# Which queue carries the loads: SyncE and ACT swap roles in a 180-degree image rotation

## The chip, the cores and the metric

The kernel runs on one core of a Trainium2 chip. DMA transfers are issued from SyncE and from ACT (ScalarE), each through a queue of its own: on the profile's page q1 is SyncE's queue and q10 is ACT's (50.07 and 0.26 MB in the kernel before). VectorE does the copies. The metric is device time in microseconds (us); the profiled span is about 1.8 us shorter. The kernel before takes 122.06 us (median of 3 runs, 121.93 to 122.1).

## The reference

```python
def setup_inputs():
    batch, c, h, w = 32, 3, 256, 256
    return {"x": np.random.randn(batch, c, h, w).astype(np.float32)}

def reference(x):
    return np.rot90(x, k=2, axes=(-2, -1)).astype(np.float32)
```

A rotation by 180 degrees reverses each of the 96 planes of 65,536 floats from end to end: 25.17 MB in, 25.17 MB out, no arithmetic.

## The kernel before

The planes are taken in three groups of 32, A, B and C. Each plane is cut into four strips of 64 KB, so a group fills 128 partitions with 64 KB each. VectorE reverses each strip in place, through a scratch tile, in 12 copies, and the store writes the four strips of a plane in reverse order.

```python
    def load(t, g, lo, hi, queue=nc.sync):
        return queue.dma_start(out=t[:, lo:hi], in_=x4[g][:, lo:hi])
    def store(t, g, lo, hi):
        return nc.sync.dma_start(out=o4[g][:, ::-1, lo:hi], in_=t[:, lo:hi])
    # ... inside(t): the 12 copies ...
    TAIL = 1536
    HEAD = 512
    load(A, 0, 0, HEAD, nc.scalar)          # head: 2 KB a row, on ACT's queue
    load(A, 0, HEAD, E)                     # bulk of A: 62 KB a row
    load(Bt, 1, 0, E)
    body = load(Ct, 2, 0, E - TAIL)
    load(Ct, 2, E - TAIL, E)                # tail: 6 KB a row
    inside(A)
    LEAD = 128
    store(A, 0, 0, LEAD)                    # lead: 512 B a row
    first = store(A, 0, LEAD, E)            # held until body has landed
    # ... the manual dependency of first on body ...
    for g, t in ((1, Bt), (2, Ct)):
        inside(t)
        store(t, g, 0, E)
```

The large store of A waits by hand for the body of C (32.5 us in the profile), so that it doesn't compete with the loads. The small lead and the tail of C bridge the time in which that store is being issued: it is issued at 59.63 us and its first packet starts at 60.84, and the lead's packets start between 60.48 and 61.22.

Of the kernel before, what the change touches and what calls it, by code (L numbers as in the profile page):

```python
# [2 lines left out]

os.environ.setdefault("NEURON_RT_ULTRASERVER_MODE", "4")

# [4 lines left out]


@with_exitstack
def kernel(
    ctx: ExitStack,
    tc: tile.TileContext,
    x: bass.AP,
    out: bass.AP,
):








    nc = tc.nc
    P = 128

    B, C, H, W = x.shape
    L = H * W
    G = 32
    E = L // 4
    J = E // 8

    x4 = x.rearrange("b c h w -> (b c) (h w)").rearrange(
        "(g n) (s e) -> g (n s) e", n=G, s=4)
    o4 = out.rearrange("b c h w -> (b c) (h w)").rearrange(
        "(g n) (s e) -> g n s e", n=G, s=4)  # L40

    pool = ctx.enter_context(tc.tile_pool(name="slots", bufs=1))
    A = pool.tile([P, E], x.dtype, tag="A")
    Bt = pool.tile([P, E], x.dtype, tag="B")
    Ct = pool.tile([P, E], x.dtype, tag="C")
    T = pool.tile([P, J], x.dtype, tag="T")

    def back(t, lo, hi):
        return t[:, hi - 1:(lo - 1 if lo else None):-1]

    def copy(dst, src):
        tc.keep_in_program_order(nc.vector.tensor_copy(out=dst, in_=src))  # L52

    def load(t, g, lo, hi, queue=nc.sync):
        return queue.dma_start(out=t[:, lo:hi], in_=x4[g][:, lo:hi])  # L55

    def store(t, g, lo, hi):
        return nc.sync.dma_start(
            out=o4[g][:, ::-1, lo:hi], in_=t[:, lo:hi])

    def inside(t):
        for lo in range(0, E // 2, J):
            hi = E - lo - J
            copy(T[:, :], back(t, hi, hi + J))
            copy(t[:, hi:hi + J], back(t, lo, lo + J))
            copy(t[:, lo:lo + J], T[:, :])

    TAIL = 1536
    HEAD = 512
    load(A, 0, 0, HEAD, nc.scalar)  # L70
    load(A, 0, HEAD, E)
    load(Bt, 1, 0, E)
    body = load(Ct, 2, 0, E - TAIL)
    load(Ct, 2, E - TAIL, E)
    inside(A)
    LEAD = 128
    store(A, 0, 0, LEAD)
    first = store(A, 0, LEAD, E)
    tc.add_manual_dep(
        first.ins, body.ins.name,  # L80
        mybir.DependencyInfo(mybir.DependencyClass.Sync, mybir.DependencyReason.DATA),
        reason="the first store is queued while the last strip is on its way")
# [5 lines that stand above are left out]
# [1 line left out]
_INS = ['x']  # L89
_OUTS = [((32, 3, 256, 256), 'float32')]  # L90


# [23 lines left out]
```

## Time and profile before

| | before |
|---|---|
| device time | 122.06 us |
| profiled span | 120.2 us |
| VectorE busy | 44.2 us (37%) |
| data moved | 50.33 MB, 419 GB/s over the span |
| share of queue q1 (SyncE) / q10 (ACT) | 97.0% / 0.6% |

A DMA "packet" in what follows is one row's contiguous piece: the page's 1296 packets are 128 for each of the nine DMAs and 144 under 512 bytes. 128 rows over 16 DMA engines make 8 packets per engine on average for each DMA.

### The profile page before, as it was taken

What the parts mean: (1) busy time and instruction counts of PE and PEld (TensorE: products, weight loads), DVE (VectorE), ACT (ScalarE), POOL (GpSimd) and SP (SyncE); (2) the same over time, 40 slices, a digit from 0 to 9 for tenths busy, and PEclk for the clock granted to TensorE, in tenths of its full rate; (3) what the DMA queues carried; (4) which work ended last, traced back from release to release, by engine and by line L of the source; (5) the groups of instructions that cost most, each with busy time, mean ns of one, the idle gap of its engine ahead of it and who ended that gap; (6) DMA issues with size and microseconds to landing.
All of it is one profiled execution on the core that took longest, in us unless ns stands there. A gap on an engine that the chain in (4) does not pass through costs nothing.

```text
span 120.2 us, 97 instructions
## 1 busy us (share of the span) xinstructions
DVE 44.2 (37%) x36; POOL 0.2 (0%) x4
## 2 busy tenths in 40 slices
DVE  0000000499995099999059999500000000000000
POOL 0000000000000000000000000000000000000000
DMA  9888988899889879979499777988898889888990
GB/s 338 349 349 349 698 349 349 360 654 393 349 349 633 382 316 553 395 316 633 178 452 693 346 346 346 693 349 349 349 698 349 349 349 698 349 349 349 654 393 0
DMA packets 1296, 50.33 MB, mean 419 GB/s; under 512 B 144, under 2 KB 272, under 8 KB 528
## 3 DMA queue, kind: packets, MB, share of 16 engines
q1 hardware_dynamic: 1152, 50.07, 97.0%
q10 hardware_dynamic: 144, 0.26, 0.6%
HBM read 25.17 MB, written 25.17 MB: 419 GB/s over the span
## 4 chain that ended last, share of the span: by engine, by line
DMA 34%; DVE 25%; another core or an unknown queue 4%; issue 1%; SPq 0%; DVEq 0%
DMA Bt<-in_x_dram 34%; DVE T L52 8%; DVE Bt L52 8%; DVE Ct L52 8%; SPq L55 0%; DVEq L52 0%
## 5 line engine op out<-in xcount | busy, mean ns | idle before, releaser
L52 DVE COPY T<-A 128x2048 f32<-128x2048 f32 x4 | 4.9, 1226 | 22.7 <-DMA A<-in_x_dram 22.6
L52 DVE COPY T<-Ct 128x2048 f32<-128x2048 f32 x4 | 4.9, 1227 | 4.5 <-DMA Ct<-in_x_dram 4.4
L52 DVE COPY T<-Bt 128x2048 f32<-128x2048 f32 x4 | 4.9, 1226 | 4.4 <-DMA Bt<-in_x_dram 4.3
L52 DVE COPY Bt<-Bt 128x2048 f32<-128x2048 f32 x4 | 4.9, 1227 | 0.1
L52 DVE COPY A<-A 128x2048 f32<-128x2048 f32 x4 | 4.9, 1227 | 0.1
L52 DVE COPY A<-T 128x2048 f32<-128x2048 f32 x4 | 4.9, 1227 | 0.1
L52 DVE COPY Bt<-T 128x2048 f32<-128x2048 f32 x4 | 4.9, 1227 | 0.1
L52 DVE COPY Ct<-T 128x2048 f32<-128x2048 f32 x4 | 4.9, 1227 | 0.1
L52 DVE COPY Ct<-Ct 128x2048 f32<-128x2048 f32 x4 | 4.9, 1227 | 0.1
L100 POOL MEMSET const-bfloat16-1.0<- 128x1 bf16 x1 | 0.1, 101 | 0.0
L100 POOL MEMSET const-uint8-127<- 128x1 uint8 x1 | 0.1, 101 | 0.0
L100 POOL MEMSET const-float32-0.0<- 128x1 f32 x1 | 0.1, 98 | 0.2 <-issue 0.2
L100 POOL MEMSET const-float32-1.0<- 128x1 f32 x1 | 0.1, 98 | 0.0
## 6 DMA issues: line engine op xcount, KB each, us to landing
out_dram<-A SPq DMA_DIRECT2D x1, 8128.0 KB, 21.1
A<-in_x_dram SPq DMA_DIRECT2D x1, 7936.0 KB, 21.9
Ct<-in_x_dram SPq DMA_DIRECT2D x1, 7424.0 KB, 57.9
Ct<-in_x_dram SPq DMA_DIRECT2D x1, 768.0 KB, 59.3
A<-in_x_dram ACTq DMA_DIRECT2D x1, 256.0 KB, 22.0
out_dram<-A SPq DMA_DIRECT2D x1, 64.0 KB, 35.2
Bt<-in_x_dram SPq DMA_DIRECT2D x1, 40.8
out_dram<-Bt SPq DMA_DIRECT2D x1, 39.8
```

Of the source, the lines that this page charges most:

```text
L52: tc.keep_in_program_order(nc.vector.tensor_copy(out=dst, in_=src))
L100: nc = _bacc.Bacc("TRN2", target_bir_lowering=False, num_devices=1)
```

## The change

The intent is to give loads and stores a queue each, so that no store stands behind a load, as the lead store did for 35.2 us in the kernel before. ACT carries the bulk of the loads, SyncE the head of A and all stores. The calls are pinned in program order, which does not alter the order of the stores.

```diff
-    def load(t, g, lo, hi, queue=nc.sync):
-        return queue.dma_start(out=t[:, lo:hi], in_=x4[g][:, lo:hi])
+    def load(t, g, lo, hi, queue=nc.scalar):
+        return tc.keep_in_program_order(
+            queue.dma_start(out=t[:, lo:hi], in_=x4[g][:, lo:hi]))
 
     def store(t, g, lo, hi):
-        return nc.sync.dma_start(
-            out=o4[g][:, ::-1, lo:hi], in_=t[:, lo:hi])
+        return tc.keep_in_program_order(nc.sync.dma_start(
+            out=o4[g][:, ::-1, lo:hi], in_=t[:, lo:hi]))
...
-    load(A, 0, 0, HEAD, nc.scalar)
+    load(A, 0, 0, HEAD, nc.sync)
```

## The prediction

> **What bounds the kernel now.** I read the page's slices first. VectorE is busy in 44.2 of 120.2 us, only between the first landing and the middle of the run. The DMA engines are busy from end to end:
>
> ```profile
> DVE  0000000499995099999059999500000000000000
> ...
> DMA  9888988899889879979499777988898889888990
> ...
> DMA packets 1296, 50.33 MB, mean 419 GB/s; under 512 B 144, under 2 KB 272, under 8 KB 528
> q1 hardware_dynamic: 1152, 50.07, 97.0%
> q10 hardware_dynamic: 144, 0.26, 0.6%
> ```
>
> q1 is SyncE's queue and carries all but 256 KB; q10 is ACT's and carries only the head (2 KB of each row of group A). A packet's bytes are booked where it starts, which is why slices swing between 178 and 698 GB/s while the digits hardly fall. Is there a hole anywhere? I take the issue starts from the timeline and add the landing times of the page's sixth part:
>
> ```profile
> out_dram<-A SPq DMA_DIRECT2D x1, 8128.0 KB, 21.1
> A<-in_x_dram SPq DMA_DIRECT2D x1, 7936.0 KB, 21.9
> ...
> A<-in_x_dram ACTq DMA_DIRECT2D x1, 256.0 KB, 22.0
> out_dram<-A SPq DMA_DIRECT2D x1, 64.0 KB, 35.2
> Bt<-in_x_dram SPq DMA_DIRECT2D x1, 40.8
> ```
>
> Landings: A 0.73 + 21.9 = 22.6, B 1.18 + 40.8 = 42.0, C's tail 2.1 + 59.3 = 61.4; stores A 59.6 + 21.1 = 80.7, B 60.3 + 39.8 = 100.1, C 76.7 + 42.7 = 119.4. The steps are 19.4, 19.4, 19.3, 19.4 and 19.3 us for 8.39 MB each: 433 GB/s, for loads, for stores, and across the turn from one to the other. So the run is 22.6 (start-up plus the first group) + 5 x 19.36 + 0.8 after the last landing = 120.2. There is no idle stretch to win back except the start-up, 22.6 - 19.4 = 3.2 us. The chain that ended last stops at VectorE's last copy at 76.7; that store then waits behind two others, so the copies are not the limit: C's store is issued at 76.7 and its turn comes at 100.
>
> The waits of SyncE show the timing of the turn:
>
> ```profile
> SPq L58 <- DMA Ct<-in_x_dram: 33.1, 2, 32.5
> ...
> SPq L58 <- DVE A L52: 3.6, 1, 3.6
> ```
>
> The large store of A is held 32.5 us for the body of C, issued at 59.63, and its packets start 1.2 us later. Windows around that point (start:end, length, VectorE, POOL, clock, DMA share, GB/s):
>
> ```profile
> 60.00:60.45 0.45, 0.00 (x0) 0.00 (x0) 1.00 0.98 410
> 60.45:60.84 0.39, 0.00 (x0) 0.00 (x0) 1.00 0.82 313
> 60.84:61.06 0.22, 0.00 (x0) 0.00 (x0) 1.00 7.42 3105
> 61.06:61.26 0.20, 0.00 (x0) 0.00 (x0) 1.00 4.67 1997
> ```
>
> The jump at 60.84 is the first 65,024-byte store packets. Before it the share falls only to 0.82: a few early engines ran dry, for 0.18 x 0.39 = 0.07 us on average. The late engines reached the store only after 61.06, with it already waiting. The late ones set the end.
>
> [...]
>
> ```profile
> DMA packets 16, 1.02 MB, mean 317 GB/s; under 512 B 0, under 2 KB 0, under 8 KB 0
> ...
> q1 hardware_dynamic: 16, 1.02, 94.9%
> ```
>
> That is 1.5 to 4.7 us: one 63,488-byte packet on each of 16 engines and none of the head. From 4.7 to 5.2 us:
>
> ```profile
> q1 hardware_dynamic: 13, 0.83, 380.6%
> q10 hardware_dynamic: 15, 0.03, 15.8%
> ```
>
> Now one head packet per engine goes between two large ones. A head has 8 packets per engine (128 rows over 16), so it needs 8 turns and lands after 22.0 us, with the whole of A (21.9), though 256 KB alone would need 0.6 us at 433 GB/s.
>
> **The change, part by part.** Nothing is removed or added in work. The instruction order shows the same 36 copies on VectorE with the same kinds of wait, and the same nine DMAs of the same sizes: SyncE now has the head and four stores, ACT four loads. The order on SyncE is as before: lead (first 512 B of each row of A), rest of A, B, C. So 50.33 MB at 433 GB/s stay.
>
> (1) *Start.* Both sequencers begin at 0.73 us, ACT's issue takes 0.38 us and SyncE's 0.39, so ACT issues its four loads at the pace at which SyncE did. Each engine still has 8 large and 8 head packets before group B. If SyncE's head wins the first turn, the order in each pair is swapped and the head meets the start-up latency instead of the large packet: 2,048 bytes took 0.08 us in the packet records, so the effect is within +-0.1 us. If ACT's descriptors should come later than SyncE's, the engines pass the time with head packets, 8 x 0.08 = 0.67 us of useful work. Cost 0, at most 0.3.
>
> (2) *The lead store.* Before, it is issued at 26.4 and waits behind B and C in the same queue, until 61.6 (35.2 us). Now its queue is empty, so it takes a turn at once: 8 packets, one for each large load packet (65,536 bytes, 2.42 us), so about 8 x 2.42 = 19.4 us, up to 2.4 more for the first turn. It lands some 20 us after its issue. Its packets are 0.0235 us apart in the packet records, so 8 are 0.19 us per engine: spent in the load phase instead of at the turn. C's body lands 0.2 us later, the turn is 0.2 us shorter: sum 0.
>
> (3) *The turn.* The lead no longer stands between C's tail and the large store. The store is issued at about 59.8 and starts at about 61.0. The tails end, shifted by 0.19, between 60.67 (from 60.48) and 61.24 (from 61.05). The earliest engine now idles some 0.36 us, where before it idled 0.17; the latest has its store waiting, as before. So the end stays, unless the store's arrival slips. On late engines a 6,144-byte tail packet or the tail's completion can be left when the store comes in, and then stands behind one or two packets of 2.4 us. The tail may thus land at 61.6 to 66.5, and VectorE's C copies (15.1 us) end at 77 to 82. C's store has its turn at 100: 18 us of slack. Hidden.
>
> (4) *Stores B and C* queue behind A on SyncE, as now.
>
> Sum: 0 from the data, 0 to +0.3 at the start, 0 to +0.2 at the turn.
>
> **The rivals.** *Turns cost something.* If the switch between two queues cost a gap, or made loads and stores mix badly, the lead's 8 turns would pay it. Against: the head already makes 128 such turns and A's group costs 22.6 us, of which start-up explains the 3.2. At 0.1 us a turn it would be 0.8 us: 122.9. *A bubble at the turn.* If the store's packets came 1 us later through the changed queue, all engines would idle: 123. Against: the same sequencer, the same wait on C's body. *A starved tail.* With the tail's 8 small packets all alternating with 2.4 us stores it would take some 20 us, C would be ready at about 97, still just before 100; only with this and a delay would the end move, by 1 to 3 us. Against: the body's completion and the 1.2 us to the first packet leave at most one tail packet. *A gain.* Earlier stores can't help, because the large store is still held for C's body; a head that hides start-up latency could give 0.1 to 0.3 us, 121.8.
>
> **Range and chances.** The runs before spread over 121.93 to 122.1. I take 122.1, with 121.6 to 122.6 for the small terms and the difference from chip to chip. Over 2% is 2.4 us, more than any rival but two at once: faster 0.01, within 2% 0.97, slower 0.02.
>
> **What would show it.** Span 120.0 to 120.6; q10 carries about 24.9 MB and q1 about 25.4; lead store about 20 us to landing; large store of A issued at 59.7 to 59.9 and landing 21 us on; first copy of A at 22.5 to 22.9; first copy of C at 61.6 to 66.5; C's store landing at 119.3 to 119.8. I am wrong if group A comes 1 us or more late (ACT's issue path), if the steps of 19.36 us change (turns cost), or if the DMA digits show a hole at 58 to 63 us.

## The result, and the profile after

The changed kernel takes 122.59 us (median of 6 runs, 122.29 to 122.71); the kernel before took 122.01 (6 runs, 121.93 to 122.1). The ratio is 1.0045, with a 95% interval of 1.0032 to 1.0058. A ratio is the mean time of one kernel's fast runs over the mean of the other's fast runs of the same rounds, so it is not quite the ratio of the medians. The 0.45%, about 0.55 us, is clear of noise.

The page of the kernel after: busy tenths of the DMA engines in 40 slices, and the two queues (packets, MB, share of the 16 engines' span).

```profile
DMA  8988997899889979979599877988898889888990
...
q1 hardware_dynamic: 720, 25.43, 49.3%
q10 hardware_dynamic: 576, 24.90, 47.9%
```

The traffic is divided as expected and there is still no hole. The page's DMA issues (size, us from issue to landing):

```profile
out_dram<-A SPq DMA_DIRECT2D x1, 8128.0 KB, 21.0
A<-in_x_dram ACTq DMA_DIRECT2D x1, 7936.0 KB, 22.4
...
A<-in_x_dram SPq DMA_DIRECT2D x1, 256.0 KB, 20.0
out_dram<-A SPq DMA_DIRECT2D x1, 64.0 KB, 22.3
Bt<-in_x_dram ACTq DMA_DIRECT2D x1, 41.4
```

The lead store lands 22.3 us after its issue instead of 35.2, so it does go early. But the bulk of A took 22.4 us instead of 21.9, B 41.4 instead of 40.8, and the head landed 2 us sooner (20.0 against 22.0). The delay is there before group A has landed and stays to the end. VectorE's first copy starts at 23.12 instead of 22.62, B's at 42.68 instead of 42.05, C's at 62.12 instead of 61.55.

So I look at the first microseconds. Windows (start:end, length, VectorE, POOL, clock, DMA share, GB/s), first before, then after. A packet's bytes and its whole time are booked where it starts, so a share can exceed 1 and is no measure of how busy the engines are within the window:

```profile
1.50:2.10 0.60, 0.00 (x0) 0.00 (x0) 1.00 4.82 1587
2.10:2.85 0.75, 0.00 (x0) 0.00 (x0) 1.00 0.20 85
2.85:4.00 1.15, 0.00 (x0) 0.00 (x0) 1.00 0.00 0
```

```profile
1.50:2.10 0.60, 0.00 (x0) 0.00 (x0) 1.00 1.23 270
2.10:2.85 0.75, 0.00 (x0) 0.00 (x0) 1.00 2.01 625
2.85:4.00 1.15, 0.00 (x0) 0.00 (x0) 1.00 0.92 392
```

Before, 15 of the 16 first large packets start before 2.10 us (1587 GB/s x 0.60 us = 952 KB, 15 packets of 63,488 bytes). After, they trickle in until past 2.85 us. The queue view of the changed kernel from 1.5 to 4.0 us says what went ahead of them:

```profile
q10 hardware_dynamic: 16, 1.02, 102.0%
q1 hardware_dynamic: 32, 0.07, 30.0%
```

There are 32 head packets, two per engine on average (the records don't name the engine), and one large packet each. Before, the large packet was first on every engine (16 packets on q1 and none on q10 from 1.5 to 4.0 us). The packet records show what the head packets cost here: 0.08 to 1.14 us each (mean 0.38), where a head packet later in the stream takes 0.084. The first large packets start between 2.06 and 3.54 us (mean 2.79), before between 1.76 and 2.82 (mean 1.93).

A second thing in the same lines matters for the account below. The 16 large packets took 102.0% of 2.5 us, 2.55 us on average; before, 94.9% of 3.2 us (the line is in the prediction), 3.04 us. The same size takes 2.34 us later in the stream. So the head packets took a part of the start-up time off the large packets behind them, and the average engine lost little: it begins B at 22.20 instead of 21.98. What grew more is the spread over the engines.

The engines are spread more widely when they begin group B. Windows around that moment, before and after:

```profile
21.62:22.25 0.63, 0.00 (x0) 0.00 (x0) 1.00 4.00 1717
22.25:22.85 0.60, 0.23 (x1) 0.00 (x0) 1.00 0.00 0
```

```profile
21.62:22.25 0.63, 0.00 (x0) 0.00 (x0) 1.00 2.41 1040
22.25:22.85 0.60, 0.00 (x0) 0.00 (x0) 1.00 1.52 655
```

Before, all engines have begun B by 22.25; after, six have not (655 x 0.60 = 393 KB, six packets of 64 KB). By the packet records, the latest engine begins B at 22.75 instead of 22.24, which is 0.51 us later. The end of the last store packet is 119.59 instead of 119.06, which is 0.53 us later. In this profiled run the whole loss is there at 22.75.

The turn to the stores moves with it. Windows of the kernel after:

```profile
60.40:60.84 0.44, 0.00 (x0) 0.00 (x0) 1.00 0.93 391
60.84:61.30 0.46, 0.00 (x0) 0.00 (x0) 1.00 0.42 174
61.30:61.72 0.42, 0.00 (x0) 0.00 (x0) 1.00 5.88 2492
```

The jump of the large store's first packets stands after 61.30 (61.42 by the packet records) instead of at 60.84, since the body of C, for which it waits, is complete only when the latest engine has finished. Just before it the earlier engines ran dry: by the packet records' real times the 16 engines were busy for 0.57 of the window 60.84 to 61.30 (before, for all of it), and from 58 to 64 us each engine idled 0.32 us on average. Is this a second loss, or only the first one seen again? That, and whether the queue split costs anything of itself, is for experiments.

### The profile page after: what moved, and what is told of

Read it like the earlier page. It is cut to its first block, busy times and chain, and to the rows that moved or that the text cites. A ratio compares the mean times of both kernels' runs of the same rounds, so it can differ in the third digit from the quotient of the medians.

```text
span 120.7 us, 97 instructions
## 1 busy us (share of the span) xinstructions
DVE 44.2 (37%) x36; POOL 0.2 (0%) x4
## 2 busy tenths in 40 slices
DMA packets 1296, 50.33 MB, mean 417 GB/s; under 512 B 144, under 2 KB 272, under 8 KB 528
## 4 chain that ended last, share of the span: by engine, by line
DMA 34%; DVE 25%; another core or an unknown queue 3%; issue 1%; ACTq 0%; DVEq 0%
DMA Bt<-in_x_dram 34%; DVE T L52 8%; DVE Ct L52 8%; DVE Bt L52 8%; ACTq L56 0%; DVEq L52 0%
## 6 DMA issues: line engine op xcount, KB each, us to landing
A<-in_x_dram ACTq DMA_DIRECT2D x1, 7936.0 KB, 22.4
Ct<-in_x_dram ACTq DMA_DIRECT2D x1, 768.0 KB, 59.9
out_dram<-A SPq DMA_DIRECT2D x1, 64.0 KB, 22.3
Bt<-in_x_dram ACTq DMA_DIRECT2D x1, 41.4
out_dram<-Bt SPq DMA_DIRECT2D x1, 39.8
```

## The experiments

Theory S is that the loss comes from the start: SyncE's small head packets get to the DMA engines ahead of ACT's large ones. Rival Q is that loads and stores taking turns between two queues cost it. Rival A is that ACT's queue is slow to start by itself. Diffs are against the changed kernel unless said otherwise. All outputs were correct. One execution of each kernel was profiled, and it isn't always a typical one; its time stands in the table at the end of this section. Up to four kernels shared runs of the kernel before (medians 122.02, 122.04 and 122.08).

**Swap without split**

```diff
-        return tc.keep_in_program_order(nc.sync.dma_start(     # in store()
+        return tc.keep_in_program_order(nc.scalar.dma_start(
```

> The swap without the split: head on SyncE, all other loads and all stores on ACT in one queue. Theory S (the 0.6 us arises at the start, because SyncE's head packets reach the DMA engines before ACT's bulk packets): 122.5 to 122.7, first copy of A at 23.1, lead store landing 34 to 36 us after issue. Rival Q (the cost is in loads and stores taking turns between two queues: lead in the load phase, and the turn at 60 us): 122.0, first copy of A at 22.6.

Measured: 122.29 (122.13 to 122.51), ratio 1.0025 (1.0012 to 1.0037), some 0.3 us. The profiled run was the slowest of the set, 122.51. Its queue view from 1.5 to 4.0 us:

```profile
q10 hardware_dynamic: 16, 1.02, 99.6%
q1 hardware_dynamic: 48, 0.10, 32.1%
```

Here it is three head packets per engine on average ahead of the large one, and the first copy of A at 23.21. Loads and stores share one queue, the lead lands 35.2 us after issue as before, and still time is lost. S stands in kind; the size is less than it said, and Q, which said 122.0, can't be the cause of this part.

**Split without swap**

```diff
-    def load(t, g, lo, hi, queue=nc.scalar):
+    def load(t, g, lo, hi, queue=nc.sync):
-        return tc.keep_in_program_order(nc.sync.dma_start(     # in store()
+        return tc.keep_in_program_order(nc.scalar.dma_start(
-    load(A, 0, 0, HEAD, nc.sync)
+    load(A, 0, 0, HEAD, nc.scalar)
```

> The split without the swap: head on ACT and all loads on SyncE as before, only the four stores moved to ACT. Theory S: 121.9 to 122.2, first copy of A at 22.6, although the lead store goes early (about 22 us to landing). Rival Q: 122.5 to 122.7 with the first copy of A still at 22.6 and the loss at 59 to 62 us.

Measured: 122.16 (122.1 to 122.29), ratio 1.0014 (1.0000 to 1.0027). First copy of A at 22.61, lead landing 22.3 us after issue. This is within S's range and far below Q's. The ratio means 0.17 us for the split, and by the interval anything from none to 0.33 us.

**Changed kernel without a head**

```diff
-    load(A, 0, 0, HEAD, nc.sync)
-    load(A, 0, HEAD, E)
+    load(A, 0, 0, E)
```

> The changed kernel with A loaded by one DMA on ACT, no head on SyncE. Theory S: 121.9 to 122.2, first packets of ACT's queue at 1.7 to 2.1 us and first copy at 22.6. Rival A (ACT's queue is slow to deliver its first packets, whatever SyncE does): 122.5, first ACT packets later than 2.1 us and spread, first copy at 23.1. Rival Q: 122.5 with the first copy at 22.6.

Measured: 122.04 (122.04 to 122.17), ratio 1.0005 (0.9992 to 1.0017). The queue view from 1.5 to 4.0 us:

```profile
q10 hardware_dynamic: 16, 1.05, 125.4%
```

ACT's 16 large packets start at 1.74 to 2.15 us when nothing is ahead of them, and the first copy comes at 22.58. ACT's queue is not slow, so A falls. The stores are still in their own queue, the lead still goes early (22.2 us to landing), and the loss is gone to within the interval's 0.2 us, so Q falls again as the main cause.

**Head held back**

```diff
+    nc.gpsimd.memset(A[:, 0:HEAD], 0.0)
     load(A, 0, 0, HEAD, nc.sync)
```

> The changed kernel, but SyncE's head is held back by a GpSimd memset of its 2 KB columns, so that ACT's bulk is first on the engines. Theory S: 121.9 to 122.2, the first packets are 63,488 bytes, first copy of A at 22.6 to 22.8. Rival A: 122.5, ACT's first packets late though alone. Rival Q: 122.5.

Measured: 122.14 (122.06 to 122.37), ratio 1.0014 (1.0001 to 1.0026). The profiled run was the fastest of the set, 122.06. SyncE's issue moves from 0.73 to 1.28 us. The first packets are then 63,488 bytes on every engine (1.74 to 2.57 us), the first copy comes at 22.50, and the time is 0.4 us under the changed kernel's. The same DMAs on the same queues, in the other order, are without most of the loss (the intervals of the two ratios don't meet). The order is the cause of most of it.

**Kernel before without its head** (against the kernel before)

```diff
-    load(A, 0, 0, HEAD, nc.scalar)
-    load(A, 0, HEAD, E)
+    load(A, 0, 0, E)
```

> The kernel before without its head on ACT: A is one DMA on SyncE, everything in one queue. Theory S (only heads that come before the bulk cost anything; the head on ACT in the kernel before is harmless and useless): 121.9 to 122.15, first copy of A at 22.5 to 22.6. Rival H (the head on the other queue won the kernel before something at the start): 122.3 or more, first copy at 22.9.

Measured: 122.06 (121.97 to 122.62), ratio 1.0012 (0.9995 to 1.003). Four of the six runs are at 121.97 to 122.08, two at 122.46 and 122.62. By the median the head in the kernel before is neither gain nor loss. The profiled run was the one of 122.62, and in it one engine began B at 22.52, the next at 22.22, with no small packet at the start; one first packet took 3.50 us and ended at 5.61, where the mean is 5.02. So an engine can fall behind at the start for other reasons too; whether the head makes this rarer, six runs don't say.

**A larger head**

```diff
-    HEAD = 512
+    HEAD = 4096
```

> The changed kernel with a head of 16 KB a row instead of 2 KB (about 0.6 us a packet at the rate of the large ones). Theory S1 (small packets at the start each pay their own latency, and larger ones hide it): at most two head packets per engine before the first bulk packet, 122.0 to 122.25. Rival G (ACT's bulk descriptors come late beside SyncE's, whatever the heads do, and the engines idle for them): with 0.6 us of work per head packet the wait is covered by one packet; one head before the bulk on most engines, again 122.0 to 122.25, so the time does not part them but the count does. Rival T (any two queues at the start cost): 122.5 to 122.7.

Measured: 122.18 (122.05 to 122.39), ratio 1.001 (0.9998 to 1.0023). One head packet per engine ran ahead of the bulk on all 16, and it took 0.81 to 1.74 us where the later ones took 0.61. The large packet followed without a gap. Time and count fit both S1 and G, so this run didn't tell them apart. It does show where the start-up time goes: the first head packet took 1.25 us on average, 0.64 more than later ones, and the large packet behind it 1.84, hardly more than the 1.81 of later ones. So the start-up was paid once, by the packet that came first.

**A longer tail**

```diff
-    TAIL = 1536
+    TAIL = 3072
```

> The changed kernel with C's tail doubled from 6 KB to 12 KB a row, so that the large store of A is issued about 1.9 us earlier and no engine waits for it. Theory M (the store phase evens the engines out, so the end follows the mean start of the store and the idle 0.22 us per engine at the turn counts): 122.3 to 122.4. Rival L (only the latest engine counts, as the prediction had it): 122.5 to 122.7. In both the tail lands late, at 65 to 75 us, since its packets take turns with the store's, and the copies of C end before 95.

Measured: 122.59 (122.55 to 123.01), ratio 1.0055 (1.004 to 1.007): no gain. The start of the last store packets, first in this run, then in the changed kernel:

```profile
116.30:116.67 0.37, 0.00 (x0) 0.00 (x0) 1.00 3.68 1594
116.67:117.30 0.63, 0.00 (x0) 0.00 (x0) 1.00 0.96 416
```

```profile
116.30:116.67 0.37, 0.00 (x0) 0.00 (x0) 1.00 0.00 0
116.67:117.30 0.63, 0.00 (x0) 0.00 (x0) 1.00 3.85 1664
```

With the longer tail nine engines start their last packet in the first window (1594 x 0.37 = 590 KB), where the changed kernel has none, and only four start in the second (three started before). The wait at the turn is gone and most engines finish early, but the latest ends at 119.64, as late as in the changed kernel. So M falls and L stands: the idle time at the turn is the first loss seen again. Both had the tail wrong: it landed at 2.1 + 60.0 = 62.1 us, not at 65 to 75, although the store was issued at 58.29. The tail's packets all went first.

**Two tests of how the head delays the bulk.** Rival G says that ACT's rows are ready late because SyncE's are made first, whatever the engines do with them.

```diff
-    load(A, 0, 0, HEAD, nc.sync)
-    load(A, 0, HEAD, E)
+    D = pool.tile([P, 128], x.dtype, tag="D")
+    nc.sync.dma_start(out=D[0:127, :], in_=x4[0][0:127, 0:128])
+    load(A, 0, 0, E)
```

> The changed kernel with SyncE's head replaced by a load that nobody reads, 127 rows of 512 bytes, and A whole on ACT. [...] SyncE still issues nearly as many rows at the same moment, but 15 engines get no small packets. Theory S1 (the small packets on the engine itself delay the bulk): the bulk's first packets start at 1.74 to 2.15 us on 15 engines, as when ACT was alone, and late on one. Rival G (ACT's bulk rows come late because SyncE's are made first, by whatever they share): they start at 2.1 to 3.5 us on all 16. The one engine has some 3.4 us more to do, so the time is 123 to 126 in either case and says nothing; only the packets' starts count.

Measured: one run, 124.66. The first large packets start at 1.75 to 2.06 us on 12 engines, at 2.32 to 2.47 on three, and at 3.71 on the last. 46 small packets went ahead of that one (21 of them between 1.7 and 2.2 us, one every 0.024 us), and none starts between it and 4.0 us, so the small packets stood on its engine. That is S1's picture, a little wider than it said; the three are within what is seen with no small packet in front (2.82 in the kernel before). G wanted 2.1 to 3.5 us on all 16 and falls.

```diff
-    load(A, 0, 0, HEAD, nc.sync)
-    load(A, 0, HEAD, E)
+    D = pool.tile([P, HEAD], x.dtype, tag="D")
+    nc.sync.dma_start(out=D[0:16, :], in_=x4[0][0:16, 0:HEAD])
+    load(A, 0, 0, E)
```

> The changed kernel with SyncE's head cut to 16 rows of 2 KB that nobody reads (one small packet per DMA engine, 2 KB each), A whole on ACT. Theory S1: one small packet instead of two before the bulk, so about half the loss, 122.1 to 122.4, or none where the bulk's row comes first. Rival G: with an eighth of the rows to make, the bulk starts at 1.75 to 2.1 and the time is 122.0 to 122.15. Neither: 122.5 or more.

Measured: 122.24 (122.16 to 122.51), ratio 1.0014 (1.0001 to 1.0028). The profiled run, the slowest of the set, has one small packet per engine at the start, of 0.08 to 0.72 us, and large packets from 1.84 to 3.17 us. One small packet instead of two costs less (122.24 against 122.59), as S1 said.

**A try at beating both** (against the kernel before)

```diff
-    load(A, 0, 0, HEAD, nc.scalar)
-    load(A, 0, HEAD, E)
+    nc.sync.dma_start(out=A[0:16, :], in_=x4[0][0:16, :])
+    nc.sync.dma_start(out=A[16:P, :], in_=x4[0][16:P, :])
```

> A try at beating both: the kernel before without a head, and group A loaded in two DMAs on SyncE, rows 0 to 15 first (one packet per engine), then rows 16 to 127. If the 1.0 us from issue to first packet grows with the number of descriptors, the first packets start before 1.6 us and the run takes 121.6 to 121.9; if it is a fixed latency, they start at 1.75 as before and the run takes 121.9 to 122.2.

Measured: 143.94 (143.21 to 144.11), ratio 1.1778. The windows of its start:

```profile
1.50:3.00 1.50, 0.00 (x0) 0.00 (x0) 1.00 5.79 699
3.00:9.00 6.00, 0.00 (x0) 0.00 (x0) 1.00 0.00 0
```

The first packets start at 1.74 us, as they do with 128 rows and nothing ahead of them (1.73 to 1.76), so here the time from issue to first packet didn't depend on the number of rows. But each packet then takes 7.7 to 9.3 us instead of 3.04 (the mean in the kernel before), and the first copy comes at 44.95. By the packet records the first DMA's 1.05 MB ran from 1.74 to 11.26 us, 110 GB/s, against the 433 of the kernel before. The other 112 rows were slow too: the whole of A landed at 44.9 us (1.17 + 43.7) instead of 22.6. Why both were slow, no run here shows. No version tried beats the kernel before.

**All together.** From the packet records (us, to about 0.01); each row is the profiled run, whose own time stands in the last column, and ratios are from all fast runs:

```
kernel                first large packet     latest engine   last store    ratio     run us
                      min / mean / max       begins B        packet ends
before                1.76 / 1.93 / 2.82     22.24           119.06        1         121.97
after                 2.06 / 2.79 / 3.54     22.75           119.59        1.0045    122.53
swap without split    2.11 / 2.84 / 3.70     22.82           119.58        1.0025    122.51
split without swap    1.73 / 1.87 / 2.31     22.24           119.23        1.0014    122.16
no head               1.74 / 1.90 / 2.15     22.21           119.09        1.0005    122.04
head held back        1.74 / 1.90 / 2.57     22.18           119.04        1.0014    122.06
head of 16 KB         2.87 / 3.23 / 3.61     22.37           119.25        1.0010    122.18
tail of 12 KB         2.02 / 2.73 / 3.44     22.64           119.64        1.0055    122.57
before without head   1.74 / 1.89 / 2.35     22.52           119.67        1.0012    122.62
one small packet      1.84 / 2.32 / 3.17     22.50           119.60        1.0014    122.51
```

The end comes 96.8 to 97.2 us after the latest engine begins B in every row. So that moment settles the end to within 0.4 us, and between the kernels before and after to 0.03: enough for their difference of 0.5 us, not for one of 0.1 or 0.2. The runs with one engine's head and with the first 16 rows are left out.

## Why the prediction was right or wrong

The prediction of 122.1 us with a range of 121.6 to 122.6 held, at the very edge: 122.59, and "within 2%" was right. That it held is in part luck: the start cost more than the most that the prediction gave it, and the range was kept because the rest of the sum stayed near zero.

- **The bound.** Right. That 433 GB/s would stay was an estimate from a trace with nearly everything on one queue (50.07 of 50.33 MB on q1); with two queues stores and loads still run at the same rate (the issues and landing times of the changed kernel put its landings 19.2 to 19.5 us apart, 430 to 437 GB/s), 50.33 MB have still to pass, and splitting the queues won nothing.
- **(1) Start, "Cost 0, at most 0.3".** This term was mis-sized: it was about 0.5 us in the profiled run, and 0.3 us where the swap was made alone. It failed in "2,048 bytes took 0.08 us in the packet records". That duration is from the steady stream. As the first packets on an engine the same 2,048 bytes took 0.08 to 1.14 us, and two of them on average, not one, ran ahead. The idea that the head meets the start-up latency instead of the large packet was right in part: two head packets took 0.75 us, where "useful work" would have been 0.17, but the large packet behind them took 0.49 less (2.55 instead of 3.04). What the term lacked is that this is paid unequally: the average engine begins B 0.22 us later, the latest 0.51, and the latest counts. The head was without much cost here only where the bulk came first, in the kernel before (122.04, and 122.06 without the head) and with the head held back (122.14).
- **(2) The lead store.** Right: it no longer waited for B and C (issued at 26.90, its packets start between 31.39 and 46.61 us, before between 60.48 and 61.22) and landed after 22.3 us ("some 20" was expected, from 19.4 and up to 2.4 more; it is 0.5 above that sum).
- **(3) The turn.** Right in its claim that the latest engine sets the end; the longer tail shows it. The 0.07 us of idle time that it read from a window's share of 0.82 was a misreading, since a share is booked where packets start: the packet records give 0.01. Its times are off by what the start had cost: the large store was issued at 60.2, not 59.8, with packets from 61.42; with the head held back it was issued at 59.67 and with no head at 59.73. The tail was not held up: C's first copy came at 62.12, at the early end of 61.6 to 66.5. The split alone reads 0.14% (0.00 to 0.27%), 0.17 us; "0 to +0.2" covers that, not the whole interval.
- **(4) Stores B and C.** Right: they land 39.8 and 42.7 us after issue, as before.
- **The rivals.** Turns that cost something fall, with the split alone, and with the changed kernel without its head, at 122.04 with the lead still taking its turns. The bubble at the turn fell: the large store's packets follow its issue by 1.20 us (60.22 to 61.42), before by 1.21 (59.63 to 60.84). The gain from hiding start-up latency in the head fell as a gain: the head took part of that latency off the large packets, 0.49 us on average, but cost more than that itself.
- **The signs named.** Of seven, three held: the bytes per queue, the lead and the first copy of C. The large store's held by half: 21.0 us to landing, but issued at 60.22 instead of 59.7 to 59.9. Outside their ranges were the span (120.7 against 120.0 to 120.6), the first copy of A (23.12 against 22.5 to 22.9) and the landing of C's store (77.25 + 42.7 = 119.95 against 119.3 to 119.8). All three point to the start. For a group A that comes late (it said 1 us or more; it was 0.5) the prediction named "ACT's issue path"; the reason is instead what stood ahead of ACT's packets on the engines.

What stays open: why a load of 16 rows ran at 110 GB/s; why a small packet takes up to 1.14 us at the start, and why the engines differ so; whether the split of the queues costs 0.1 to 0.3 us or nothing; and why the swap alone read 0.25% where the whole change read 0.45% (their intervals, 1.0012 to 1.0037 and 1.0032 to 1.0058, do overlap). Swap and split alone come to 0.39% together, so a small cost of the split beside that of the start is not excluded.

## What to carry to other kernels

In a kernel that keeps the DMA engines full, ask of each queue what it puts on an engine first: large packets first and small ones behind cost nothing here (122.04 with such a head, 122.06 without), small ones first cost about half a microsecond in the changed kernel, and that is kept to the end. The latest of the 16 engines set the time here, and the last of the first large packets started 1.06 us behind the earliest before (2.82 against 1.76) and 1.48 us after (3.54 against 2.06). So look at the spread over the engines and not only at mean bandwidth. A packet's duration from the steady stream was no measure of the same packet at the start: 0.084 us against a mean of 0.38.
